# Three tiles of weights split early, and worked together, where two layers begin behind a norm

## The chip, the cores and the metric

One core of a Trainium2 chip runs the whole program. The metric is the device time of one execution in microseconds (us), taken as the median over several runs.

## The reference, cut to what matters

Two blocks act on 512 tokens of width 1024: the first is a pooling layer, a latent attention layer and a final norm; the second modulates its norms with a vector `ada` and holds an attention mixer, an RWKV mixer and a feed-forward network (FFN). Two places matter here, the beginnings of the two stages that follow a modulated norm:

```
x   = rmsnorm(x + y @ w_out, final_norm)              # end of the first block
h   = rms_norm(x, norm1_w) * (1 + sc1) + sh1          # head one begins behind this norm
proj = h @ w_in                                       # its first three column tiles: the low-rank inputs of RWKV
...
x   = x + gt1 * ((g_att*y_att + g_rwkv*y_rwkv) @ w_o)
h   = rms_norm(x, norm2_w) * (1 + sc2) + sh2          # head two begins behind this norm
u   = h @ w_up                                        # then a causal convolution of width 3 over the tokens
u   = conv_b + sum(conv_w[j] * shift(u, 2-j))
out = x + gt2 * ((silu(gate) * val) @ w_down)
```

## The kernel before

Activations lie transposed, as eight pages of 128 features by 512 tokens. Every fp32 product is made of three matmuls (`mm3`, L168 to L170) over a high and a low part of both operands: hi·hi, lo·hi and hi·lo. A weight tile is 128 x 1024 (eight blocks of 128 x 128, one for each page of the activations). `wload` brings it into `wraw` (three buffers), ScalarE writes the rounded copy `whi` (L152) and VectorE the remainder `wlo` (L153), each with two buffers; these two instructions carry a high priority, so that they run as soon as a buffer is free. `gemm_n` makes one output tile in a PSUM bank: `mm`, `sc`, `tr` and `ch` are four tags of two banks each.

The program is written in order; a scheduler at compile time fixes the order of each engine's queue from that order, priorities and its own idea of what is ready. At run time every queue is worked in its fixed order, with semaphores between the engines. All weight loads are issued by SP, in order.

The two stages ahead of the heads are gemms that update the residual stream. Ahead of head one it is the output projection of the latent attention (`w_mout`, 512 input rows at a time), ahead of head two it is `w_o`. Both end in `gemm_tail`: the last tiles are worked first for tokens 0 to 255, then for 256 to 511 (`HALVES`), so that the first half's norm can begin while the second is multiplied. The norm sums squares with ones-matmuls (`norm_sum`, L254), takes a square root on ScalarE (`norm_end`, L270) and a reciprocal, and copies the result over the partitions with a matmul (`spread`, L285). `modulate` then makes a page's `mod` (L730, VectorE), `hh` (L731, ScalarE) and `hl` (L735, VectorE) for 256 tokens. In `Block2In.finish`, which feeds head one, three pages of eight in each half take another path (`pool=True`): a second ScalarE instruction (L733) and the subtraction on GpSimd (L734).

`gemm_head` makes the first tiles behind the norm. It loads two weight tiles with the remainder `wlo` taken on GpSimd, and multiplies them in halves, all eight pages for one tile and then for the other. The tiles in `more` follow in full width in the `sc` banks: one in head one (`w_rw` tile 26, loaded by `wload`), two in head two (`w_up` tiles 2 and 3, of which the first is split into four pages of its own, with GpSimd's subtraction, L219 and L220). `feat` (L808, L809) and `conv` (L1472 to L1474) empty the banks.

Of the kernel before, what the change touches and what calls it, by code (L numbers as in the profile page):

```python
# [9 lines left out]
AF = mybir.ActivationFunctionType  # L10
ALU = mybir.AluOpType
AX = mybir.AxisListType
PSUM = bass.MemoryType.PSUM
P = 128
S = 512
D = 1024
# [25 lines left out]
FULL = slice(0, S)  # L42
# [7 lines left out]
def f(ap):  # L50
    return ap.bitcast(F32)


class Kern:
# [147 lines left out]
                self.gemm_w(w, acts, ps[:, 0:S // 2], ts)  # L202
                evac(n, ps[:, 0:S // 2], ts)

    def gemm_head(self, wname, chunks, kts, acts, more=(), page=None):

        ws = []
        for c in chunks:
            ws.append(self.wchunks(wname, c, kts, self.nc.gpsimd))

        extra = None
        if page is not None:
            nc = self.nc
            raw = self.wp.tile([P, D], F32, name="wraw", tag="wraw")
            nc.sync.dma_start(raw, self.a[wname][more[0]][:, :D])
            extra = []
            for h in range(2):
                hi, lo, r = page(F32R, "xwh"), page(F32R, "xwl"), raw[:, h * S:h * S + S]
                nc.scalar.activation(hi, r, AF.Copy)  # L219
                nc.gpsimd.tensor_tensor(lo, r, f(hi), ALU.subtract)  # L220
                extra.append((hi, lo, 4))
        out = [self.mm() for _ in chunks]
        for ts in HALVES:
            for w, ps in zip(ws, out):
                self.gemm_w(w, acts, ps[:, ts], ts)
        for c in more:
            ps = self.bank("sc")
            self.gemm_w(extra or self.wchunks(wname, c, kts), acts, ps)
            extra = None
            out.append(ps)  # L230
        return out

    def gemm_multi(self, wname, chunk, kt, nt, acts, evac, n0):
# [234 lines left out]
def mla_layer(K, xs, mi, z_scr, done, after, filler=lambda h: None):  # L468

    nc = K.nc  # L470
# [3 lines left out]
    inv = K.rstd_page(mi.acc.last(), D)  # L474
# [20 lines left out]
    ps = proj(5)  # L495
# [3 lines left out]
    for i in range(4):  # L499
        j = i ^ 1  # L500
# [16 lines left out]
    for t in range(16):  # L517
        ps = proj(6 + t)
# [143 lines left out]
    def project(q, c, ys):  # L662

        K.gemm_multi("w_mout", 4 * q + c, 4, 2, ys[4 * q:4 * q + 4], evac_last if q == 3 else evac_x, 2 * c)
# [22 lines left out]
            project(q, c, ys)  # L687
    for c in range(2):
        project(3, c, ys)
    ws = []  # L690
    for c in (2, 3):
        wh, wl = K.wload("w_mout", 12 + c, D)
# [29 lines left out]
    nc.vector.scalar_tensor_tensor(K.A2, K.ada[:, 32:40], 1.0, K.v("norm2_w", 0, 8), ALU.add, ALU.mult)  # L722


def modulate(K, x, A, inv, sh, hl, ts=FULL, pool=False):

    nc = K.nc
    t = K.page(name="mod")[:, ts]
    hi, lo = hl[0][:, ts], hl[1][:, ts]
    nc.vector.scalar_tensor_tensor(t, x[:, ts], A, inv, ALU.mult, ALU.mult)  # L730
    ins = nc.scalar.activation(hi, t, AF.Identity, bias=sh)  # L731
    if pool:
        nc.scalar.activation(t, t, AF.Identity, bias=sh)  # L733
        return ins, nc.gpsimd.tensor_tensor(lo, t, f(hi), ALU.subtract)  # L734
    return ins, nc.vector.scalar_tensor_tensor(lo, t, sh, f(hi), ALU.add, ALU.subtract)  # L735


class Block2In:
# [10 lines left out]
    def finish(self):  # L749

        K, xs = self.K, self.xs
        nc = K.nc
        fa = K.const.tile([P, 8], F32, name="fa1")
        nc.vector.tensor_tensor(fa, K.A1, K.v("final_norm", 0, 8), ALU.mult)
        hs = [(K.apage("hh"), K.apage("hl")) for i in range(DT)]
        r1s = K.const.tile([P, 4], F32, name="r1s")
        hh = []
        for h, ts in enumerate(HALVES):

            nps = K.norm_sum([self.s1.last(), self.s2.last()], ts)  # L760
            ss = K.sm.tile([P, 2], F32, name="ss", tag="ss")
            with K.tc.high_priority():
                ins = nc.vector.tensor_scalar(ss, nps[:, 0:2], EPS, EPS * EPS * D, ALU.mult, ALU.add)
                for a in hh[2:3]:
                    K.behind(ins, a[1])
                nc.vector.tensor_tensor(ss, ss, nps[:, 2:4], ALU.add)
            r12 = K.norm_end(ss, D, 2, 0.0, [a[0] for a in hh[1:2]])
            inv12 = K.spread(r12, 2)
            nc.vector.tensor_copy(r1s[:, 2 * h:2 * h + 2], nps[:, 0:2])
            for i in range(DT):  # L770
                hh.append(modulate(K, xs[i], fa[:, i:i + 1], inv12, K.ada[:, i:i + 1], hs[i], ts, i in ((2, 4, 6), (1, 3, 5))[h]))
        r1s = K.norm_end(r1s, D)
        inv1 = K.spread(r1s)
        for i in range(DT):
            xf = K.page(name="xf")
            nc.vector.scalar_tensor_tensor(xf, xs[i], K.v("final_norm", i), inv1, ALU.mult, ALU.mult)
            nc.sync.dma_start(K.x_scr[i], xf)
        return hs


def rwkv(K, hs, filler=lambda: None):
    nc = K.nc
    c = K.const
# [17 lines left out]
    def feat(n, ps=None):  # L801

        if ps is None:
            ps = K.mm()
            K.gemm_n("w_rw", n, [8], hs, ps)
        z = K.page(name="zm")
        with K.tc.high_priority():
            nc.scalar.activation(z, ps, AF.Copy, scale=omu[:, n:n + 1])  # L808
            nc.vector.scalar_tensor_tensor(z[:, 1:], ps[:, :S - 1], K.v("mu", n), z[:, 1:], ALU.mult, ALU.add)  # L809
        return z  # L810

    pss = K.gemm_head("w_rw", (24, 25), [8], hs, (26,))
    zs_ = [feat(24 + i, ps) for i, ps in enumerate(pss)]

    lw = zs_[0]
    nc.scalar.activation(lw[0:64], lw[0:64], AF.Tanh)
# [30 lines left out]
    for i in range(2):  # L847

        wh, wl = K.wload("w_g2", i, 8 * P)
        raw = K.wraw.rearrange("p (u q c) -> p u q c", u=4, q=2)[64:128, :, 1]  # L850
        w4 = wh.rearrange("p (u q c) -> p u q c", u=4, q=2)[64:128, :, 1]
        nc.vector.tensor_tensor(w4, raw, f(w4), ALU.subtract)
        for u in range(4):
            ps = K.mm()
# [324 lines left out]
    for b in range(4):  # L1179
# [12 lines left out]
        if b < 3:  # L1192
            i = 2 * b + 2
# [238 lines left out]
def attn_out(K, mg, xscr):  # L1432

    nc = K.nc
    xs, xf = [], []
    acc = Sums(K)
    for n in range(DT):
        t = K.page(name="xf")
        nc.sync.dma_start(t, xscr[n])
        xf.append(t)  # L1440
        xs.append(K.page(name="x"))

    def evac(n, ps, ts=FULL):
        nc.vector.scalar_tensor_tensor(xs[n][:, ts], ps, K.ada[:, 16 + n:17 + n], xf[n][:, ts], ALU.mult, ALU.add)
        acc.add(n, xs[n], ts=ts)

    for n in range(DT - 2):
        ps = K.mm()
        K.gemm_n("w_o", n, [8], mg, ps)
        evac(n, ps)  # L1450
    K.gemm_tail([(n, K.wchunks("w_o", n, [8])) for n in (DT - 2, DT - 1)], mg, evac, acc.last())
    return xs, acc


def ffn(K, xs, acc):

    nc = K.nc
    hs = [(K.apage("hh"), K.apage("hl")) for i in range(DT)]
    for ts in HALVES:
        inv = K.rstd(acc.last(), D, ts)  # L1460
        for i in range(DT):
            modulate(K, xs[i], K.A2[:, i:i + 1], inv, K.ada[:, 24 + i:25 + i], hs[i], ts)

    def conv(n, ps=None):

        ci = (n % 2) * 22 + n // 2
        if ps is None:
            ps = K.mm()
            K.gemm_n("w_up", n, [8], hs, ps)
        t = K.page(name="cv")  # L1470
        w = [K.v("conv_w", j * 44 + ci) for j in range(3)]
        nc.scalar.activation(t, ps, AF.Identity, scale=w[2], bias=K.v("conv_b", ci))  # L1472
        nc.vector.scalar_tensor_tensor(t[:, 1:], ps[:, :S - 1], w[1], t[:, 1:], ALU.mult, ALU.add)
        nc.vector.scalar_tensor_tensor(t[:, 2:], ps[:, :S - 2], w[0], t[:, 2:], ALU.mult, ALU.add)  # L1474
        return t

    pss = K.gemm_head("w_up", (0, 1), [8], hs, (2, 3), K.page)
    for half in range(2):
        act = []
        for i in range(11):  # L1480
            n = 2 * (half * 11 + i)
            gt = conv(n, pss[n] if n < 4 else None)
            vl = conv(n + 1, pss[n + 1] if n < 4 else None)
            sg = K.page(name="sg")
            nc.scalar.activation(sg, gt, AF.Silu)
            a = K.page(name="fa")
            nc.vector.tensor_tensor(a, sg, vl, ALU.mult)
            act.append(K.split(a, "fa"))
        if half == 0:
            out = []  # L1490
            for n in range(DT):
                ps = K.mm()
                K.gemm_n("w_down", 2 * n, [6, 5], act, ps)
                x = K.page(name="x")
                nc.vector.scalar_tensor_tensor(x, ps, K.ada[:, 40 + n:41 + n], xs[n], ALU.mult, ALU.add)
                out.append(x)
            xs = out
    acc = Sums(K)
    xw = [K.page(name="xw") for n in range(DT)]

    def evac(n, ps, ts=FULL):
        x = xs[n][:, ts]
        nc.vector.scalar_tensor_tensor(x, ps, K.ada[:, 40 + n:41 + n], x, ALU.mult, ALU.add)  # L1503
        acc.add(n, xs[n], ts=ts)
        nc.gpsimd.tensor_scalar(xw[n][:, ts], x, K.v("norm_f_w", n), None, ALU.mult)

    for n in range(DT - 1):
        ps = K.mm()
        K.gemm_n("w_down", (DT + n) * 2, [6, 5], act, ps)
        evac(n, ps)  # L1510
    K.gemm_tail([(DT - 1, K.wchunks("w_down", (2 * DT - 1) * 2, [6, 5]))], act, evac, acc.last())
    return xw, acc
# [293 lines left out]
```

## Time and profile before

| | |
|---|---|
| median of 3 runs | 1997.57 us (1993.21 to 1999.24) |
| the profiled execution | 1998.78 us, of which its span is 1997.0 us |
| TensorE (PE) | 1932.4 us busy, 97% |
| VectorE (DVE) | 1273.2 us, 64% |
| ScalarE (ACT) | 892.4 us, 45% |
| GpSimd (POOL) | 111.0 us, 6% |
| mean granted TensorE clock | 0.993 of full speed |

Head one lies near 758 to 787 us of the span, head two near 1616 to 1647 us. A busy share is an average over stages; what a head is worth is read in its own stretch. In a timeline each row has the start, the duration, the engine, the line, the output and inputs, and in brackets how long the engine was idle before it and what ended that.

### The profile page before, as it was taken

To read this page: it belongs to the slowest core of one execution; us is meant where nothing else is said; L and a number is where in the kernel's file an instruction comes from. 1 tells how busy PE (TensorE), PEld (TensorE's weight loads), DVE (VectorE), ACT (ScalarE), POOL (GpSimd) and SP (SyncE) were. 2 spreads that over 40 slices of the span, in tenths; PEclk is the share of its full clock that TensorE was granted. 3 is DMA by queue.
4 is the path that set the end of the run, shared out by engine and by line. 5 is a ranking of instruction groups with operands and counts; after the bars stand their busy time and mean duration, and the time that the engine had idled before them with its cause. 6 is when DMAs were issued, how large, how long until landed. Compare 5 with 4: busy or idle time off the path is not lost. (4 is left out here: it accounts for less than half of the span.)

```text
span 1997.0 us, 28388 instructions
## 1 busy us (share of the span) xinstructions
PE 1932.4 (97%) x10771; PEld 1561.6 (78%) x10771; DVE 1273.2 (64%) x2284; ACT 892.4 (45%) x1618; POOL 111.0 (6%) x221
## 2 busy tenths in 40 slices
PE   8999999999999998999999999989999999999998
PEld 6888887887888887777777767767777888888886
DVE  6746777768866668675576576566465566635555
ACT  5322333336655545544545655655552344423432
POOL 0000000000000002110020020020000010000002
PEclk9999999999999999999999999999999999999999
DMA  4332365685422223643443433333554423233322
GB/s 163 98 103 96 95 198 182 208 233 178 129 85 74 82 64 127 207 124 111 152 136 101 149 102 131 133 127 106 180 191 148 153 75 96 82 99 108 101 79 90
DMA packets 97496, 254.55 MB, mean 127 GB/s; under 512 B 11216, under 2 KB 15824, under 8 KB 97360
## 3 DMA queue, kind: packets, MB, share of 16 engines
q1 hardware_dynamic: 96848, 251.51, 39.5%
q8 instruction: 85, 1.39, 0.3%
q0 software_dynamic: 224, 0.79, 0.1%
q10 hardware_dynamic: 288, 0.45, 0.1%
q14 instruction: 51, 0.42, 0.1%
HBM read 212.59 MB, written 37.75 MB: 125 GB/s over the span
## 5 line engine op out<-in xcount | busy, mean ns | idle before, releaser
L152 ACT ACTIVATE whi<-wraw 128x1024 fp32r<-128x1024 f32 (+4 forms) x302 | 299.3, 991 | 609.1 <-PE mm L169 393.7
L153 DVE TENSOR_TENSOR wlo<-wraw,whi 128x1024 fp32r<-128x1024 f32 (+4 forms) x298 | 338.4, 1136 | 191.2 <-ACT whi L152 188.8
L169 PE MATMUL mm<-hl,whi 128*128 128x512 f32 (+1 forms) x992 | 390.1, 394 | 4.0 <-DVE hl L735 3.6
L168 PE MATMUL mm<-hh,whi 128*128 128x512 f32 (+1 forms) x992 | 388.5, 393 | 0.7 <-DVE zm L809 0.7
L170 PE MATMUL mm<-hh,wlo 128*128 128x512 f32 (+1 forms) x992 | 387.4, 391 | 0.1
L169 PEld LDWEIGHTS mm<-hl,whi 128*128 128x128 f32 x992 | 188.1, 190 | 43.1 <-DVE hl L735 4.4
L168 PEld LDWEIGHTS mm<-hh,whi 128*128 128x128 f32 x992 | 188.1, 190 | 41.2 <-issue 4.2
L170 PEld LDWEIGHTS mm<-hh,wlo 128*128 128x128 f32 x992 | 188.3, 190 | 37.8 <-issue 2.8
L168 PE MATMUL mm<-xgh,whi 128*128 128x512 f32 x432 | 170.5, 395 | 7.5 <-ACT xgh L334 7.0
L169 PE MATMUL mm<-xgl,whi 128*128 128x512 f32 x432 | 171.4, 398 | 0.8 <-DVE xgl L335 0.8
L170 PE MATMUL mm<-xgh,wlo 128*128 128x512 f32 x432 | 169.4, 392 | 0.0
L168 PEld LDWEIGHTS mm<-xgh,whi 128*128 128x128 f32 x432 | 82.0, 190 | 25.5 <-ACT xgh L334 7.0
L168 PE MATMUL mm<-yh,whi 128*128 128x512 f32 (+1 forms) x256 | 98.3, 384 | 0.0
L169 PE MATMUL mm<-yl,whi 128*128 128x512 f32 (+1 forms) x256 | 98.0, 383 | 0.0
L170 PE MATMUL mm<-yh,wlo 128*128 128x512 f32 (+1 forms) x256 | 98.0, 383 | 0.0
L169 PEld LDWEIGHTS mm<-xgl,whi 128*128 128x128 f32 x432 | 82.2, 190 | 19.4 <-DVE xgl L335 1.7
L170 PEld LDWEIGHTS mm<-xgh,wlo 128*128 128x128 f32 x432 | 82.0, 190 | 17.9 <-issue 1.0
L712 DVE SCALAR_TENSOR_TENSOR adaw<-adaw,cb 128x1024 f32<-128x1024 f32 x48 | 58.7, 1222 | 34.7 <-DMA adaw<-in_w_ada 33.7
L170 PE MATMUL mm<-fah,wlo 128*128 128x512 f32 (+1 forms) x176 | 67.3, 382 | 0.0
L169 PE MATMUL mm<-fal,whi 128*128 128x512 f32 (+1 forms) x176 | 67.3, 382 | 0.0
L168 PE MATMUL mm<-fah,whi 128*128 128x512 f32 (+1 forms) x176 | 67.3, 382 | 0.0
L650 ACT ACTIVATE p<-sc,nm 128x128 f32<-128x128 f32 (+1 forms) x64 | 33.8, 527 | 57.9 <-DVE nm L647 43.7
(423 smaller groups left out, 3583.3 us busy)
## 6 DMA issues: line engine op xcount, KB each, us to landing
adaw<-in_w_ada SPq DMA_DIRECT2D x48, 512.0 KB, 3.9
wraw<-in_w_up SPq DMA_DIRECT2D x44, 512.0 KB, 3.6
wraw<-in_w_at SPq DMA_DIRECT2D x36, 512.0 KB, 3.7
wraw<-in_w_pin SPq DMA_DIRECT2D x32, 512.0 KB, 3.5
wraw<-in_w_rw SPq DMA_DIRECT2D x27, 512.0 KB, 4.1
wraw<-in_w_min SPq DMA_DIRECT2D x22, 512.0 KB, 4.1
a_scr<-aqkv SPq DMA_DIRECT2D x36, 256.0 KB, 2.4
aq<-a_scr SPq DMA_DIRECT2D x36, 256.0 KB, 3.8
```

The source lines that it names most:

```text
L152: nc.scalar.activation(hi, raw, AF.Copy)
L153: eng.tensor_tensor(lo, raw, f(hi), ALU.subtract)
L168: nc.tensor.matmul(out, wh, ah, start=first, stop=False)
L169: nc.tensor.matmul(out, wh, al, start=False, stop=False)
L170: nc.tensor.matmul(out, wl, ah, start=False, stop=last)
L650: nc.scalar.activation(p[:, :nk], sc[:, :nk], AF.Exp, bias=nm, scale=scale, accum_out=sm)
L712: nc.vector.scalar_tensor_tensor(w, w, 1.0, K.cb, ALU.mult, ALU.mult, accum_out=K.ada[:, i:i + 1])
```

## The change

`gemm_head` loses its loads. A new `head_weights` brings three tiles into `wraw` and splits each into four pages from the page pool, with the remainder on VectorE and without the high priority. It is called earlier in the program: for `w_rw` tiles 24 to 26 behind the second `project` call and ahead of the loads of the last two `w_mout` chunks, for `w_up` tiles 0 to 2 ahead of the loads of the last two `w_o` tiles. `gemm_head` then goes, in each half of the tokens, page by page through all three tiles (nine matmuls for each page), into two `mm` banks and one `sc` bank; tile 3 of `w_up` is an ordinary `gemm_n` behind it. In head one the call moves from the start of `rwkv` into `Block2In.finish`, ahead of the last norm of that function. GpSimd's path in `modulate` goes away.

```
+    def head_weights(self, wname, chunks, page):
+        ws = []
+        for c in chunks:
+            raw = self.wp.tile([P, D], F32, name="wraw", tag="wraw")
+            nc.sync.dma_start(raw, self.a[wname][c][:, :D])
+            w = []
+            for h in range(2):
+                hi, lo, r = page(F32R, "xwh"), page(F32R, "xwl"), raw[:, h * S:h * S + S]
+                nc.scalar.activation(hi, r, AF.Copy)
+                nc.vector.tensor_tensor(lo, r, f(hi), ALU.subtract)
+                w.append((hi, lo, 4))
+            ws.append(w)
+        return ws
+    def gemm_head(self, ws, acts):
+        out = [self.mm(), self.mm(), self.bank("sc")][:len(ws)]
         for ts in HALVES:
-            for w, ps in zip(ws, out):
-                self.gemm_w(w, acts, ps[:, ts], ts)
-        for c in more:
-            ps = self.bank("sc")
-            self.gemm_w(extra or self.wchunks(wname, c, kts), acts, ps)
+            for ci in range(2):
+                for j in range(4):
+                    sl = slice(j * P, (j + 1) * P)
+                    k = ci * 4 + j
+                    for w, ps in zip(ws, out):
+                        hi, lo, _ = w[ci]
+                        self.mm3(ps[:, ts], hi[:, sl], lo[:, sl], acts[k][0][:, ts], acts[k][1][:, ts], k == 0, k == 7)
...
     for c in range(2):
         project(3, c, ys)
+    K.head = K.head_weights("w_rw", (24, 25, 26), K.page)
...
-    if pool:
-        nc.scalar.activation(t, t, AF.Identity, bias=sh)
-        return ins, nc.gpsimd.tensor_tensor(lo, t, f(hi), ALU.subtract)
...
+        K.heads = K.gemm_head(K.head, hs)
         r1s = K.norm_end(r1s, D)
...
+    K.head = K.head_weights("w_up", (0, 1, 2), K.page)
     K.gemm_tail([(n, K.wchunks("w_o", n, [8])) for n in (DT - 2, DT - 1)], mg, evac, acc.last())
...
-    pss = K.gemm_head("w_up", (0, 1), [8], hs, (2, 3), K.page)
+    pss = K.gemm_head(K.head, hs)
```

## Rows read from the trace of the kernel before

**Rows 1.** The page: busy time of an engine, and one costly group.

```profile
PE 1932.4 (97%) x10771; PEld 1561.6 (78%) x10771; DVE 1273.2 (64%) x2284; ACT 892.4 (45%) x1618; POOL 111.0 (6%) x221
...
L153 DVE TENSOR_TENSOR wlo<-wraw,whi 128x1024 fp32r<-128x1024 f32 (+4 forms) x298 | 338.4, 1136 | 191.2 <-ACT whi L152 188.8
```

**Rows 2.** Windows: length, busy us of PE, PEld, DVE, ACT, POOL, then granted clock.

```profile
757.90:763.30 5.40, 0.70 (x2) 0.32 (x3) 5.40 (x13) 3.01 (x6) 2.46 (x1) 0.81 0.40 103
763.30:768.10 4.80, 4.79 (x22) 4.80 (x23) 4.80 (x16) 3.58 (x11) 1.35 (x2) 0.50 0.29 106
...
1616.00:1621.40 5.40, 2.07 (x13) 1.45 (x12) 5.40 (x8) 1.97 (x4) 3.35 (x2) 1.00 0.47 129
1621.40:1628.20 6.80, 6.80 (x32) 6.62 (x32) 3.85 (x12) 1.94 (x5) 0.00 (x0) 0.50 0.13 52
...
877.30:880.70 3.40, 3.40 (x15) 2.56 (x14) 2.67 (x4) 2.11 (x5) 0.00 (x0) 0.51 0.29 25
```

**Rows 3.** Waits of PE, 1600 to 1650 us: total, times, longest.

```profile
PE mm L169 <- DVE hl L735: 3.6, 4, 1.9
```

**Rows 4.** Timeline of PE around head one.

```profile
757.62 0.28 PE L170 MATMUL sc<-yh,wlo 128*128 128x256 f32 x1
...
763.31 0.98 PE L254 MATMUL tr<-ones,sq 128*128 128x1 f32 x4 [3.61 <-DVE sq L312]
...
786.76 0.39 PE L168 MATMUL mm<-hh,whi 128*128 128x512 f32 x1
```

**Rows 5.** Timeline of PE around head two.

```profile
1616.04 0.28 PE L168 MATMUL mm<-hh,whi 128*128 128x256 f32 x1
...
1630.97 0.28 PE L170 MATMUL mm<-hh,wlo 128*128 128x256 f32 x1
1631.09 0.28 PE L168 MATMUL mm<-hh,whi 128*128 128x256 f32 x1
...
1646.89 0.39 PE L170 MATMUL sc<-hh,wlo 128*128 128x512 f32 x1
1647.12 0.39 PE L168 MATMUL mm<-hh,whi 128*128 128x512 f32 x1
```

**Rows 6.** Timeline of POOL at head two.

```profile
1614.49 2.39 POOL L153 TENSOR_TENSOR wlo<-wraw,whi 128x1024 fp32r<-128x1024 f32 x1 [277.17 <-ACT whi L152]
1617.31 2.47 POOL L153 TENSOR_TENSOR wlo<-wraw,whi 128x1024 fp32r<-128x1024 f32 x1 [0.42 <-ACT whi L152]
```

**Rows 7.** Timeline of DVE at head two.

```profile
1614.69 2.47 DVE L312 TENSOR_TENSOR sq<-sq 128x256 f32<-128x256 f32 x1
...
1617.48 0.47 DVE L730 SCALAR_TENSOR_TENSOR mod<-x,A,ch 128x256 f32<-128x256 f32 x1
1617.88 2.18 DVE L735 SCALAR_TENSOR_TENSOR hl<-mod,ada,hh 128x256 fp32r<-128x256 f32 x1
...
1621.55 0.41 DVE L312 TENSOR_TENSOR sq<-sq 128x256 f32<-128x256 f32 x1
```

**Rows 8.** Timeline of DVE at head one.

```profile
756.42 1.46 DVE L312 TENSOR_TENSOR sq<-sq 128x256 f32<-128x256 f32 x1
...
760.28 2.16 DVE L312 TENSOR_TENSOR sq<-sq 128x256 f32<-128x256 f32 x1
```

**Rows 9.** Timeline of SP, ahead of head one: five loads issued over 26 us.

```profile
736.51 26.00 SPq L140 DMA_DIRECT2D wraw<-in_w_rw  x5
```

**Rows 10.** DMA issues: count, size, median us to landing.

```profile
wraw<-in_w_up SPq DMA_DIRECT2D x44, 512.0 KB, 3.6
```

**Rows 11.** Timeline behind the heads: the work that empties the banks.

```profile
797.66 0.74 DVE L809 SCALAR_TENSOR_TENSOR zm<-mm,vec,zm 128x511 f32<-128x511 f32 x1
...
1638.12 1.43 ACT L1472 ACTIVATE cv<-mm,vec 128x512 f32<-128x512 f32 x2
...
1640.90 1.39 DVE L1474 SCALAR_TENSOR_TENSOR cv<-mm,vec,cv 128x510 f32<-128x510 f32 x2
```

**Rows 12.** Timeline of DVE: an ordinary remainder of one page.

```profile
1663.27 0.69 DVE L163 TENSOR_TENSOR fal<-fa,fah 128x512 fp32r<-128x512 f32 x1 [0.70 <-ACT fah L162]
```

More of the change, by code (lines that the diff above doesn't have):

```diff
@@ L203, in gemm_tail @@
                 evac(n, ps[:, 0:S // 2], ts)
-    def gemm_head(self, wname, chunks, kts, acts, more=(), page=None):
+    def head_weights(self, wname, chunks, page):
+        nc = self.nc
         ws = []
         for c in chunks:
[L209 to L213, printed above, removed]
             raw = self.wp.tile([P, D], F32, name="wraw", tag="wraw")
-            nc.sync.dma_start(raw, self.a[wname][more[0]][:, :D])
-            extra = []
+            nc.sync.dma_start(raw, self.a[wname][c][:, :D])
+            w = []
             for h in range(2):
@@ L219, in gemm_head @@
                 nc.scalar.activation(hi, r, AF.Copy)
-                nc.gpsimd.tensor_tensor(lo, r, f(hi), ALU.subtract)
-                extra.append((hi, lo, 4))
-        out = [self.mm() for _ in chunks]
-        for ts in HALVES:
-            for w, ps in zip(ws, out):
-                self.gemm_w(w, acts, ps[:, ts], ts)
-        for c in more:
-            ps = self.bank("sc")
-            self.gemm_w(extra or self.wchunks(wname, c, kts), acts, ps)
-            extra = None
-            out.append(ps)
+                nc.vector.tensor_tensor(lo, r, f(hi), ALU.subtract)
[4 more added lines that the diff above has]
+        out = [self.mm(), self.mm(), self.bank("sc")][:len(ws)]
+        for ts in HALVES:
+            for ci in range(2):
[5 more added lines that the diff above has]
+                        self.mm3(ps[:, ts], hi[:, sl], lo[:, sl], acts[k][0][:, ts], acts[k][1][:, ts], k == 0, k == 7)
         return out
@@ L722, in ada_finish, with modulate @@
     nc.vector.scalar_tensor_tensor(K.A2, K.ada[:, 32:40], 1.0, K.v("norm2_w", 0, 8), ALU.add, ALU.mult)
-def modulate(K, x, A, inv, sh, hl, ts=FULL, pool=False):
+def modulate(K, x, A, inv, sh, hl, ts=FULL):
     nc = K.nc
@@ L770, in finish @@
             for i in range(DT):
-                hh.append(modulate(K, xs[i], fa[:, i:i + 1], inv12, K.ada[:, i:i + 1], hs[i], ts, i in ((2, 4, 6), (1, 3, 5))[h]))
+                hh.append(modulate(K, xs[i], fa[:, i:i + 1], inv12, K.ada[:, i:i + 1], hs[i], ts))
+        K.heads = K.gemm_head(K.head, hs)
         r1s = K.norm_end(r1s, D)
@@ L810, in feat @@
         return z
-    pss = K.gemm_head("w_rw", (24, 25), [8], hs, (26,))
-    zs_ = [feat(24 + i, ps) for i, ps in enumerate(pss)]
+    zs_ = [feat(24 + i, ps) for i, ps in enumerate(K.heads)]
     lw = zs_[0]
@@ L1481, in ffn @@
             n = 2 * (half * 11 + i)
-            gt = conv(n, pss[n] if n < 4 else None)
-            vl = conv(n + 1, pss[n + 1] if n < 4 else None)
+            gt = conv(n, pss[n] if n < 3 else None)
+            vl = conv(n + 1, pss[n + 1] if n < 2 else None)
             sg = K.page(name="sg")
```

## The prediction

> **What bounds the kernel now.** I read the page first: PE is busy 97% of the span and no other engine over 64% [rows 1], so time is to be had only where PE stands still or runs slowly. I then cut windows at the two heads, read PE's waits there, and followed the waits into the timelines of DVE and POOL. The reader should see three things.
>
> First, each head has a hole and a slow stretch behind it. At head one PE's last matmul of the stage before ends at 757.9, and the next real work is the norm sum at 763.31 [rows 4]; in these 5.4 us PE is busy 0.70, and in the 4.8 us behind them the granted clock is 0.50, the 1.2 GHz level [rows 2]. At head two PE is busy 2.07 of 5.40 us and then works 6.8 us at 0.50 [rows 2]. There it waits 3.6 us, in four waits, for `hl` [rows 3].
>
> Second, the hole at head two is made by GpSimd. Its two remainders last 2.39 and 2.47 us [rows 6]. While they run, a `sq` addition takes 2.47 us on DVE that takes 0.41 at 1621.55, and an `hl` takes 2.18 against 0.47 for the `mod` of the same shape in front of it [rows 7]. Head one has the same: `sq` additions of 1.46 and 2.16 us [rows 8].
>
> Third, no PE time is lost for the banks at the end of a head now: behind head two the fifth tile follows 0.23 us behind the last matmul of the fourth [rows 5], because the full-width tiles cover the emptying of the first two.
>
> **Part by part: the work of the heads.** A matmul of 256 columns steps 0.12 us and one of 512 steps 0.23 at full clock [rows 5]: a tile is 48 x 0.12 = 5.8 us in halves, 24 x 0.23 = 5.5 in full width. Head one runs from 757.9 to the next tile at 786.76 [rows 4], 28.9 us: 2 x 5.8 + 5.5 of work, about 2.0 of norm sums and spreads (from 0.98 at half clock for a sum and 0.70 for a spread [rows 2, 4]), 5.4 of hole, 2.4 lost by 4.8 us at half clock, and 2.0 of small waits. Head two with its four tiles runs from 1616.04 to 1647.12 [rows 5], 31.1 us: 2 x 5.8 + 2 x 5.5, 1.0 of norm, 3.6 of waits, 3.4 lost by 6.8 us at half clock, 0.5 of rest. After the change three tiles go in halves: 17.3 us, and at head two 5.5 for tile 3 behind them. That is 0.3 more for each tile that went in full width.
>
> **The remainders.** GpSimd's two whole remainders at each head block DVE no more: at head two (2.47 - 0.41) + (2.18 - 0.47) = 3.8 us of DVE, at head one (1.46 - 0.41) + (2.16 - 0.41) = 2.8 [rows 7, 8]. But the `whi` and `wlo` buffers that the old head filled just there are now filled by the tiles that follow, with their high priority, and with the remainder on DVE: two instructions of 1.14 us [rows 1] at each head, at the same places in time. At head two that is 2.3 in place of 3.8; at head one the first falls on DVE before the sums, where I count 0.2, and the second counts whole: 1.3 in place of 2.8. In the three pages of each half at head one DVE takes back an `hl` of 0.47, six in all; PE has nine matmuls, 1.08 us, for each page, against 0.94 for `mod` and `hl` on DVE [rows 5, 7], so these six cost nothing while PE stays the slower, and at most 6 x 0.47 = 2.8 if it doesn't.
>
> Waits for `hl` at head two: between 0 and today's 3.6. In the old order a page gave PE three matmuls, 0.36 us, before it wanted the next; now it gives 1.08, so PE no longer outruns DVE. I take 1.2, for the two remainders that still fall in. With that the hole shrinks from 3.3 us to scattered waits, and I take the clock as staying at 2.4 GHz there (bound: the 3.4 of today). Head one's hole: 5.4 - 2.8 + 1.3 = 3.9, between 2.6 (no remainder falls there) and 5.4. PE is then still idle nearly 4 us, so I expect the lower clock behind it: the loss lies between 0 and 3.4 (6.8 us at half clock, all of it filled with work); the nearest rows are 2.4 here and 1.7 for the 3.4 us at 877.30 [rows 2]; I take 2.0.
>
> The Trainium skill (Perfetto Trace Analysis, Optimizing Scalar/DVE Operations) speaks for the old side: if DVE is saturated, moving work to GpSimd may make sense, though it adds that the two share a port. DVE is indeed busy all 5.40 us of both holes [rows 2], but the blocked rows decide: GpSimd's help costs it 3.8 us where DVE's own two remainders cost 2.3. By the rule alone, head two would lose 2.3 us more, and the sum would be 2.3 smaller.
>
> **The banks.** Three tiles worked page by page end within six matmuls, 0.72 us, of each other, and the next tile wants an `mm` bank at once. This wait is new. At head one it needs one ACT step (about 0.7, from half of the pair's 1.43) and one DVE step of 0.74 [rows 11], less 0.72, plus some 0.2 of hand-over: 1.0. At head two it needs one ACT step and two DVE steps of 0.7 (half of 1.39) [rows 11]: 1.7 if tile 0 is emptied alone, 3.0 if the first DVE steps of all three tiles come before its second; I take 2.3.
>
> **The early splits.** Six ScalarE and six VectorE instructions a head, the latter 0.69 each [rows 12], 4.1 us. They fall into gemms of full-width tiles where PE is the slow one: each 5.5 us tile asks DVE for one remainder, 1.14, and some additions and evacuations, so I cost them at nothing. What they do hold are the three `wraw` buffers and SP's order: the last two loads of the stage before now stand behind all three of the head's, and each waits for a split. Head one's third load now takes the place in SP's order that was `w_rw` 24's, 736.51 [rows 9]. The tail's 96 matmuls of 0.12 and its sums start near 745.3. From 736.8 a load takes 3.6 [rows 10], `whi` and `wlo` some 1.1 each: ready at 742.6, 2.7 us in hand. Nothing is lost in this reading. L733's and GpSimd's work at head one go away unseen.
>
> **The sum.** Head one: 17.3 + 2.0 + 3.9 + 2.0 + 1.0 + 0.5 = 26.7 against 28.9, 2.2 us gained (of the 2.0 of small waits I keep 0.5, since those for GpSimd and for the third tile's remainder go). Head two: 17.3 + 5.5 + 1.0 + 1.2 + 2.3 + 0.5 = 27.8 against 31.1, 3.3 gained. Together 5.5. The profiled execution took 1998.8, 1.8 of it outside its span; it becomes 1993.3. It stands 1.2 above the median of the runs shown, so I say 1992. 0.3%, about what a measurement can tell from no change, is 6.0 us: the forecast lies just inside.
>
> **Rivals.** *The holes close.* If no remainder falls into head one's hole (+1.3), PE resumes early enough that the clock stays up (+2.0), and head two's waits vanish (+1.2), the gain is 10.0: 1988.8, on the median 1987.6. For it speaks that the blocked rows are the only long ones; against it that the buffers really come free in the middle of the holes, as the release of GpSimd's rows by `whi` shows [rows 6].
>
> *The waits are only renamed.* The remainders on DVE hold `hl` as long as GpSimd did (head two's waits stay 3.6, -2.4; head one's hole stays 5.4, -1.5) and the banks take their upper price (3.0 and 1.5, -1.2): 0.4 gained, 1998.4, on the median 1997.2. For it speaks that DVE is full in both holes [rows 2]. The Trainium skill has a rule on this side (Perfetto Trace Analysis, Matmuls): independent groups should rotate through the banks so that one is emptied under the next; three groups that end together give that up. The rows bear it out for the old order, which has no such wait.
>
> *The loads come late.* The splits lack the high priority. If they are queued behind the evacuation of the last full tile, near 745.5, the split of the first head tile ends at about 747.5, the tail's load lands at 751.1, and its weights are ready at 753.3, 8.0 us after PE wants them; at half clock behind so long a stop 3.4 more goes. Both places: 2 x 11.4 - 5.5 = 17.3 slower, 2016, on the median 2015. It decides once the first split ends after 739.5 (736.8 and the 2.7 in hand). Against it: the data can be there some ten microseconds earlier, with DVE and ACT idle between tiles.
>
> **Chances.** The forecast, 3 to 9 us gained (1988.5 to 1994.5), 0.55, of which 0.27 lie above 6; closed holes 0.18; renamed waits 0.15; late loads 0.12. So faster 0.27 + 0.18 = 0.45, same 0.28 + 0.15 = 0.43, slower 0.12. The range takes in the renamed waits with the spread of the runs and most of the closed holes: 1986.5 to 1999.
>
> **What would show it.** No POOL rows at the heads; no `sq` or `hl` of 256 columns over 1 us; `wlo` on DVE in both holes; PE waiting for `hl` little at head two and granted full clock there; a wait of 1 to 3 us for `zm` or `cv` in front of the next `mm` tile; none at the two tails. A hole at a tail, a slow stretch at head two, or bank waits over 3 us would make it wrong.

## The result, and the profile after

The changed kernel takes 2014.82 us (median of 6 runs, 2009.68 to 2021.68), the kernel before 1998.42 beside it (6 runs). The ratio is 1.0086, 95% interval 1.0072 to 1.0100: some 17 us slower. The prediction said 1992 and a range up to 1999; it was wrong. What came is nearly to the microsecond its third rival, late loads at both places (2015); that it came so near is partly luck, as the sums below show.

First the waits of PE in the profile after, from 715 to 800 us (head one with its tail) and from 1580 to 1670 (head two). Columns: total, times, longest.

```profile
PE mm L168 <- ACT whi L152: 8.7, 1, 8.7
PE tr L255 <- DVE sq L313: 2.5, 1, 2.5
PE mm L168 <- DVE zm L809: 0.8, 1, 0.8
...
PE mm L168 <- ACT whi L152: 8.4, 1, 8.4
PE mm L168 <- DVE cv L1474: 2.4, 1, 2.4
PE mm L168 <- ACT hh L733: 0.7, 1, 0.7
```

The two waits for `whi` are new and stand at the tails of the stages before, not at the heads. The windows say what they cost beyond the standstill (length, busy us of PE, PEld, DVE, ACT, POOL, then granted clock); the third and the last stand behind the waits at the heads and are used further down:

```profile
743.60:752.30 8.70, 0.00 (x0) 0.00 (x0) 5.72 (x11) 6.90 (x11) 0.00 (x0) 0.66 0.35 89
752.30:756.60 4.30, 4.29 (x19) 4.18 (x20) 2.79 (x3) 1.09 (x2) 0.00 (x0) 0.50 0.90 311
...
770.50:776.80 6.30, 6.17 (x29) 6.20 (x30) 6.30 (x20) 3.83 (x9) 0.00 (x0) 0.50 0.28 83
...
1607.10:1615.50 8.40, 0.03 (x1) 0.03 (x1) 5.19 (x9) 6.29 (x10) 0.00 (x0) 0.67 0.35 105
1615.50:1620.20 4.70, 4.66 (x20) 4.37 (x21) 2.40 (x2) 1.06 (x1) 0.00 (x0) 0.50 0.75 248
...
1654.20:1657.60 3.40, 3.40 (x10) 2.65 (x9) 1.95 (x3) 2.01 (x4) 0.00 (x0) 0.52 0.00 0
```

PE stands for 8.7 and 8.4 us and then works at half clock, the 1.2 GHz level, for 4.29 and 4.66 us, which loses half of that: 8.7 + 2.1 + 8.4 + 2.3 = 21.5 us for both tails. Why it stands is read from ACT's timeline at head one's tail, then a row of DVE's, and then SP's:

```profile
744.90 0.71 ACT L311 ACTIVATE sq<-x,vec 128x512 f32<-128x512 f32 x1
745.51 1.13 ACT L215 ACTIVATE xwh<-wraw 128x512 fp32r<-128x512 f32 x2
746.66 1.28 ACT L263 ACT_TABLE_LOAD   x1
...
748.06 2.17 ACT L215 ACTIVATE xwh<-wraw 128x512 fp32r<-128x512 f32 x4
751.20 1.06 ACT L152 ACTIVATE whi<-wraw 128x1024 fp32r<-128x1024 f32 x1 [0.96 <-DMA wraw<-in_w_mout]
```

```profile
746.24 1.28 DVE L216 TENSOR_TENSOR xwl<-wraw,xwh 128x512 fp32r<-128x512 f32 x2
```

```profile
724.00 11.21 SPq L211 DMA_DIRECT2D wraw<-in_w_rw  x3
747.56 2.80 SPq L140 DMA_DIRECT2D wraw<-in_w_mout  x2
```

The head's three loads are issued from 724.0 on. Their splits (`xwh` is the rounded copy, `xwl` the remainder) run from 745.51 on, right behind the last `sq` of a full tile. The first raw buffer is free when both its halves are split, at 747.52 (746.24 + 1.28), the next ones later. So the tail's two loads go out from 747.56 on, and the first `whi` starts at 751.20 for a PE that has stood since 743.6.

The heads themselves became shorter. PE's timeline, first at head one, from the last matmul of the tail to the next full tile, then at head two, from its first matmul to tile 3 and to the tile behind that:

```profile
766.91 0.28 PE L170 MATMUL sc<-yh,wlo 128*128 128x256 f32 x1
...
794.05 0.50 PE L168 MATMUL mm<-hh,whi 128*128 128x512 f32 x1 [0.85 <-DVE zm L809]
...
1630.79 0.28 PE L168 MATMUL mm<-hh,xwh 128*128 128x256 f32 x1
...
1653.07 0.47 PE L168 MATMUL mm<-hh,whi 128*128 128x512 f32 x1 [2.35 <-DVE cv L1474]
...
1660.23 0.39 PE L168 MATMUL mm<-hh,whi 128*128 128x512 f32 x1
```

Head one: 766.91 + 0.28 to 794.05 is 26.9 us, against 28.9 [rows 4]. Head two: 1630.79 to 1660.23 is 29.4, against 31.1 [rows 5]. So 3.7 us were gained at the heads and 21.5 lost at the tails, 17.8 in all, where the ratio says 17.2 (14 to 20). The rival had 5.5 gained and 22.8 lost: its gain and its loss were both too large, and the errors nearly cancel. The profiled spans differ by less, 13.6 (2010.6 against 1997.0). Of the 4.2 us between the two sums, 1.6 stand ahead of both heads (the same load of `w_mout` is issued at 701.95 before and at 700.33 after); the rest isn't traced.

What the prediction wanted to see at the heads is there. The profile page's row of busy times, then DVE's timeline at head one (its hole runs from 767.2 to 770.6) and at head two:

```profile
PE 1934.1 (96%) x10818; PEld 1567.4 (78%) x10819; DVE 1274.3 (63%) x2301; ACT 890.6 (44%) x1617; POOL 93.7 (5%) x209
```

```profile
765.38 1.22 DVE L153 TENSOR_TENSOR wlo<-wraw,whi 128x1024 fp32r<-128x1024 f32 x1 [0.53 <-ACT whi L152]
...
768.26 1.22 DVE L153 TENSOR_TENSOR wlo<-wraw,whi 128x1024 fp32r<-128x1024 f32 x1
...
1628.79 1.21 DVE L153 TENSOR_TENSOR wlo<-wraw,whi 128x1024 fp32r<-128x1024 f32 x1
1629.92 0.42 DVE L313 TENSOR_TENSOR sq<-sq 128x256 f32<-128x256 f32 x1
1630.26 0.48 DVE L734 SCALAR_TENSOR_TENSOR hl<-mod,ada,hh 128x256 fp32r<-128x256 f32 x1
```

POOL has 17 us less than in [rows 1] and none at the heads, the remainders lie on DVE at both heads, and a `sq` and an `hl` of 256 columns take 0.42 and 0.48 us where [rows 7] has 2.47 and 2.18.

### The profile page after: what moved, and what is told of

Read it like the earlier page. It is cut to its first block, busy times and chain, and to the rows that moved or that the text cites. A ratio compares the mean times of both kernels' runs of the same rounds, so it can differ in the third digit from the quotient of the medians.

```text
span 2010.6 us, 28473 instructions
## 1 busy us (share of the span) xinstructions
PE 1934.1 (96%) x10818; PEld 1567.4 (78%) x10819; DVE 1274.3 (63%) x2301; ACT 890.6 (44%) x1617; POOL 93.7 (5%) x209
## 4 chain that ended last, share of the span: by engine, by line
PE 45%; DVE 4%; ACT 2%; issue 1%; POOL 1%; DMA 0%; DVEq 0%; ACTq 0%; POOLq 0%
PE mm L168 12%; PE mm L169 12%; PE mm L170 12%; PE tr L1256 1%; PE ch L1100 1%; PE tr L1296 1%; PE ch L1084 1%; PE ch L1111 1%; PE ch L1095 1%; ACT whi L152 1%; PE tr L1284 1%; POOL nst L1001 1%; PE ch L1107 1%; PE sc L957 0%; DVE ar L932 0%
## 5 line engine op out<-in xcount | busy, mean ns | idle before, releaser
L152 ACT ACTIVATE whi<-wraw 128x1024 fp32r<-128x1024 f32 (+3 forms) x297 | 294.1, 990 | 607.3 <-PE mm L169 382.3
L153 DVE TENSOR_TENSOR wlo<-wraw,whi 128x1024 fp32r<-128x1024 f32 (+3 forms) x297 | 337.2, 1136 | 197.3 <-ACT whi L152 194.9
L168 PE MATMUL mm<-hh,whi 128*128 128x512 f32 x936 | 373.1, 399 | 3.2 <-DVE cv L1474 2.4
L169 PE MATMUL mm<-hl,whi 128*128 128x512 f32 x936 | 373.4, 399 | 0.0
L170 PE MATMUL mm<-hh,wlo 128*128 128x512 f32 x936 | 371.9, 397 | 0.0
L168 PEld LDWEIGHTS mm<-hh,whi 128*128 128x128 f32 x936 | 176.5, 189 | 43.7 <-issue 6.5
L169 PEld LDWEIGHTS mm<-hl,whi 128*128 128x128 f32 x936 | 176.4, 188 | 37.9 <-issue 2.7
L170 PEld LDWEIGHTS mm<-hh,wlo 128*128 128x128 f32 x936 | 176.3, 188 | 37.5 <-issue 2.8
L170 PEld LDWEIGHTS mm<-xgh,wlo 128*128 128x128 f32 x432 | 81.8, 189 | 17.8 <-issue 1.0
L168 PEld LDWEIGHTS mm<-yh,whi 128*128 128x128 f32 x256 | 49.0, 191 | 18.3 <-ACT whi L152 9.1
```

Source lines behind the costliest of these rows:

```text
L152: nc.scalar.activation(hi, raw, AF.Copy)
L153: eng.tensor_tensor(lo, raw, f(hi), ALU.subtract)
L168: nc.tensor.matmul(out, wh, ah, start=first, stop=False)
L169: nc.tensor.matmul(out, wh, al, start=False, stop=False)
L170: nc.tensor.matmul(out, wl, ah, start=False, stop=last)
```

## The experiments

All times are ratios to the kernel before on the same chip, with 95% intervals. The first six ask why the loads were late, the last six what the parts at the heads are worth.

**g1_own_pages.** The split pages get pages of their own (a tag `hw`), the pool twelve fewer.

```diff
-NP1=46
+NP1=34
-NP4=61
+NP4=49
-    K.head = K.head_weights("w_rw", (24, 25, 26), K.page)
+    K.head = K.head_weights("w_rw", (24, 25, 26), lambda dt, name: K.pg.tile([P, S], dt, name=name, tag="hw", bufs=12))
```

(and the same at `w_up`.)

> The changed kernel, but the twelve split pages of each head have pages of their own instead of coming from the pool that also serves the sq pages (twelve fewer in that pool). Theory (order of pages): the splits stood behind the last sq only because a pool's pages are handed out in program order; with pages of their own they are queued ahead of it, the raw buffers come free some 15 us earlier, and PE's waits for whi at the two tails (17.1 us) and the slow clock behind them (about 4.5 us) go: 2014.8 - 21.6 = 1993, between 1991 and 1997. Rival (buffers): that three raw buffers are held and filled first is enough by itself to make the tail's loads late: half or more of the 17.1 us stays, 2003 or more.

Measured: 1996.46 us, ratio 0.9986 (0.9972 to 1.0000). ACT's timeline, and behind it SP's:

```profile
729.22 1.13 ACT L215 ACTIVATE xwh<-wraw 128x512 fp32r<-128x512 f32 x2
...
734.65 1.14 ACT L215 ACTIVATE xwh<-wraw 128x512 fp32r<-128x512 f32 x2
736.35 1.15 ACT L215 ACTIVATE xwh<-wraw 128x512 fp32r<-128x512 f32 x2 [0.56 <-DMA wraw<-in_w_rw]
...
739.75 1.06 ACT L152 ACTIVATE whi<-wraw 128x1024 fp32r<-128x1024 f32 x1 [0.66 <-DMA wraw<-in_w_mout]
```

```profile
725.16 6.97 SPq L211 DMA_DIRECT2D wraw<-in_w_rw  x3
736.03 1.53 SPq L140 DMA_DIRECT2D wraw<-in_w_mout  x2
```

The first splits run 16 us earlier, the tail's loads go out at 736.03 in place of 747.56, and no wait for `whi` is left at either tail. The theory holds. That the head's loads come first and hold the three buffers costs nothing as long as the splits free them in time.

**e1_priority.** The splits under high priority, from the shared pool.

```diff
-                nc.scalar.activation(hi, r, AF.Copy)
-                nc.vector.tensor_tensor(lo, r, f(hi), ALU.subtract)
+                with self.tc.high_priority():
+                    nc.scalar.activation(hi, r, AF.Copy); nc.vector.tensor_tensor(lo, r, f(hi), ALU.subtract)
```

> The changed kernel with the splits under the same high priority that the splits of the whole tiles have; nothing else. Theory (order of pages): the place of the splits is set by the order in which the pool hands out its pages, priority doesn't move them, no change: 2014.8, between 2010 and 2020. Rival (the reason that the prediction named, lack of priority): the splits come ahead of the evacuations, the waits at the tails go, 1993 to 1997.

Measured: 2015.39 us, ratio 1.0082 (1.0065 to 1.0098); PE's wait for `whi` at head one is 8.8 us. No change: priority is not the reason.

**n1_more_pages.** `NP1=46` becomes `NP1=54`, nothing else.

> The changed kernel with 54 pages instead of 46 in the shared pool at head one; nothing else. Theory (the pages are handed out in program order, and the splits stand behind the sq pages however many there are): head one's wait for whi stays at 8 to 9 us, 2014.8, between 2010 and 2020. Rival (the pool is only full until the last evacuations have given pages back): with eight more the splits come earlier at head one, its wait for whi falls below 4 us, 2009 or less.

Measured: 2018.2 us, ratio 1.0088 (1.0068 to 1.0107), and again 8.7 us for `whi` at head one. Eight more pages don't help. Twelve more, as many as the splits take, were not run, but g1 does without the waits on 46 in all (34 and 12), so the number alone isn't the reason. What is left of the three runs is that splits which share a pool with the `sq` pages stay behind them, and splits with pages of their own don't. That the pool hands out its pages in program order is my reading of this; the hand-out itself is in no row.

**i1_own_pages_head_one.** The edit of g1 at head one alone.

> The changed kernel with own split pages at head one only; head two stays as changed. Theory (the two places are alike and add): head one's wait for whi (8.7 us) and the slow clock behind it go and head two's stay, half of the 18 us between the changed kernel and the one with own pages: 2005, between 2002 and 2008. Rival (one late tail moves the next stage, so that the price at head two depends on head one): 2000 or less, or 2011 or more.

Measured: 2006.27 us, ratio 1.0039 (1.0022 to 1.0056). Half of the gap is gone, there is no wait for `whi` at head one's tail, and head two's still has 8.2 us. The two places are alike and add.

**e3_behind_tail.** The head's loads and splits are called behind the tail's loads; the pool is shared.

```diff
-    K.head = K.head_weights("w_rw", (24, 25, 26), K.page)
     ws = []
     for c in (2, 3):
...
+    K.head = K.head_weights("w_rw", (24, 25, 26), K.page)
```

(at `w_up` the two `wchunks` of the tail are made ahead of `head_weights`.)

> The changed kernel, but the three early loads and their splits stand behind the tail's weight loads in program order (the pool is shared as in the changed kernel, so the splits still run after the last full sq). Theory (what costs is that the tail's two loads stand behind the held buffers): the waits for whi at the tails go whole, and with them the slow clock, 1993, between 1991 and 1998, though the splits run no earlier. Rival (the splits themselves, six ScalarE and six VectorE instructions in one lump behind the last evacuation, are what stops PE): the lump is still there, PE still waits 5 us or more at each tail, 2004 or more.

Measured: 2000.93 us, ratio 1.0010 (0.9996 to 1.0025). SP's timeline:

```profile
724.30 5.77 SPq L140 DMA_DIRECT2D wraw<-in_w_mout  x2
735.18 11.36 SPq L211 DMA_DIRECT2D wraw<-in_w_rw  x3
```

The splits run from 746.24 on, as late as in the changed kernel, and no wait for `whi` is left. So it isn't the late splits themselves that stop the tails: what cost was the tail's loads standing behind the buffers that they held. Late splits are not free, though, and the time is above the forecast for this run: PE now waits 3.1 us for `sq`, 1.7 for `dg` (what `spread` multiplies) and 1.1 for `hh` at head one, 5.9 where g1 has 3.9, and 2.7 for the same three at head two, where g1 has 0.4 for `hl`.

**e4_other_buffers.** The raw weights go as halves into pages of the pool; the raw buffers aren't held.

```diff
-            raw = self.wp.tile([P, D], F32, name="wraw", tag="wraw")
-            nc.sync.dma_start(raw, self.a[wname][c][:, :D])
...
+                r = page(F32, "xraw")
+                nc.sync.dma_start(r, self.a[wname][c][:, h * S:h * S + S])
```

> The changed kernel, but the early raw weights lie as halves in pages of the pool and not in the three raw buffers, in the same place in program order. Theory (held buffers): the tail's loads find a free raw buffer at once, no PE wait for whi at the tails, 1993 to 1998; six loads of half the size in place of three may come a little later for the head itself, at most 3 us each. Rival (the lump of splits): PE still waits 5 us or more at each tail, 2004 or more.

Measured: 2021.26 us, ratio 1.0108 (1.0092 to 1.0124). The theory's time fell. The rival's (2004 or more) came, but not by a lump of work at the tails. PE's wait at head one, then DVE's timeline there:

```profile
PE tr L255 <- DVE sq L313: 11.1, 1, 11.1
```

```profile
760.10 0.69 DVE L216 TENSOR_TENSOR xwl<-xraw,xwh 128x512 fp32r<-128x512 f32 x1 [1.54 <-ACT xwh L215]
762.93 1.35 DVE L216 TENSOR_TENSOR xwl<-xraw,xwh 128x512 fp32r<-128x512 f32 x2 [2.15 <-ACT xwh L215]
764.20 3.10 DVE L313 TENSOR_TENSOR sq<-sq 128x256 f32<-128x256 f32 x9
```

The tail's loads are in time (issued from 724.33 on) and no wait for `whi` is left, as the theory said. But the last halves of the head's weights are now issued at 758.35, behind other loads in SP's order, and their splits stand in the queues of ACT and DVE ahead of the squares and sums that the norm needs: both engines stand idle for the data, and nine `sq` additions are begun at 764.20 in one piece, when the last remainder is out. Here a split that was queued early and whose data came late held what stood behind it, 11.1 us of PE at head one.

**e7_no_gpsimd.** The kernel before, with one part of the change alone: GpSimd's remainders on DVE.

```diff
-            ws.append(self.wchunks(wname, c, kts, self.nc.gpsimd))
+            ws.append(self.wchunks(wname, c, kts))
...
-                nc.gpsimd.tensor_tensor(lo, r, f(hi), ALU.subtract)
+                nc.vector.tensor_tensor(lo, r, f(hi), ALU.subtract)
```

(and `modulate` without its `pool` argument.)

> The kernel before with one part of the change alone: the remainders that GpSimd computes at the heads are VectorE's, nothing else. Theory of the prediction (GpSimd blocks VectorE): the sq of 1.46, 2.16 and 2.47 us and the hl of 2.18 us go to 0.4 to 0.5, the four waits for hl at head two (3.6 us) shrink by 1.5 or more, 1 to 4 us faster, ratio 0.998 to 0.9995. Rival (VectorE is full in both holes, so what it takes back keeps PE waiting as long): the blocked rows go, the waits stay within 0.5 us, ratio 1.000 or a little above.

Measured: 1994.8 us, ratio 0.9978 (0.9964 to 0.9992). PE's waits at head two, a window of it, and last PE's wait at head one:

```profile
PE mm L169 <- DVE hl L735: 0.5, 1, 0.5
```

```profile
1622.00:1627.40 5.40, 4.08 (x26) 3.12 (x25) 5.18 (x13) 3.33 (x7) 0.00 (x0) 1.00 0.65 187
```

```profile
PE mm L168 <- DVE sq L312: 3.5, 1, 3.5
```

At head two the theory holds: the waits for `hl` fall from 3.6 [rows 3] to 0.5 us, with 0.8 of new ones for `wlo` and `whi`. PE is busy 4.08 of 5.40 us where it was 2.07, and no slow stretch follows [rows 2]. The head takes 26.2 us (1621.95 to 1648.14) in place of 31.1. At head one the rival holds: DVE is busy 4.92 of the 5.00 us from 762 to 767, PE waits 3.5 for a `sq` where it waited 3.61 [rows 4], and the head takes 28.95 us (762.04 to 790.99), as before. DVE's timeline of this run has these rows:

```profile
764.24 0.41 DVE L312 TENSOR_TENSOR sq<-sq 128x256 f32<-128x256 f32 x1
...
769.57 0.47 DVE L735 SCALAR_TENSOR_TENSOR hl<-mod,ada,hh 128x256 fp32r<-128x256 f32 x1
```

With GpSimd idle, `sq` and `hl` take 0.41 and 0.47 us where [rows 7] has 2.47 and 2.18. The `mod` at 1617.48 in [rows 7], which reads `x` and the PSUM bank `ch`, takes 0.47 in the middle of GpSimd's second remainder (1617.31 to 1619.78 [rows 6]). The Trainium skill (SBUF — State Buffer, Who interferes with whom) says that a VectorE instruction with two inputs in SBUF and a GpSimd instruction that reads SBUF can't run side by side, one of them is blocked. These rows agree: the blocked `sq` and `hl` read two pages in SBUF, the `mod` one.

**h1_free_bank.** From here on the base is g1. The tile behind each head goes into the free `sc` bank.

```diff
-            ps = K.mm()
+            ps = K.bank("sc") if n == 0 else K.mm()
```

(with `n == 3` in `conv`.)

> The kernel with own split pages, and the tile behind each head goes into the free bank of the other kind (sc) and not into a bank of the kind that the head's first two tiles fill. Theory (bank wait): PE's waits for zm (0.85 us) and cv (2.36 us) and the slow clock behind the second (1.7 us) go, 1996.5 - 4.9 = 1991.6, ratio to the kernel before 0.996. Rival (the wait only moves): the tile after that wants a bank of the first kind at once and the emptying on DVE is what is late; it then waits there, gain under 1 us, ratio 0.998 to 0.999.

Measured: 1993.43 us, ratio 0.9975 (0.9960 to 0.9991). The waits for `zm` and `cv` are gone, no new one stands at the heads, and head two has no slow stretch. Further behind head one, though, the wait mostly moves, as the rival had it: from 785 to 830 us PE waits 2.4 us for `zm` and `gt`, which empty banks, where g1 has 2.7 with its 0.85 in it. The point lies between the two expectations, and the interval allows both: the theory holds at head two, the rival in the main at head one.

**h4_second_half_by_tile.** Page by page in the first half of the tokens, one tile after the other in the second.

```diff
...
-                    for w, ps in zip(ws, out):
...
+            todo = [(k, w, ps) for k in range(8) for w, ps in zip(ws, out)]
+            for k, w, ps in sorted(todo, key=lambda t: [o is t[2] for o in out].index(True)) if ts is HALVES[1] else todo:
...
```

> The kernel with own split pages, and the three tiles of a head go page by page in the first half of the tokens as before, but one tile after the other in the second half, so that they end 2.9 us apart. Theory (the bank wait comes from the three tiles ending together): the waits for zm and cv go as with the free bank, and hl is ready in time, since DVE ends its last hl some 3 us after PE begins the second half: ratio 0.996. Rival (DVE is too late for a tile that wants all eight pages of the half at once): waits for hl of 1 us or more at each head take the place of the bank waits, ratio 0.998 or more.

Measured: 1990.81 us, ratio 0.9959 (0.9945 to 0.9973), as the theory said. No wait for a bank at either head, and 0.3 us for `hl` at head two; behind head one (785 to 830 us) PE waits 2.0 us where g1 has 2.7. The three groups that end together are the cause of the bank wait: it goes when their ends are staggered. That is in line with the rule that the prediction cited (the Trainium skill, Perfetto Trace Analysis, Matmuls: rotate the banks so that one is emptied under the next group); giving it up cost 0.85 and 2.35 us here.

**h3_calm_splits.** The splits of the first two full tiles behind each head lose their high priority.

```diff
-        with self.tc.high_priority():
+        with self.tc.high_priority() if self.calm < 0 else contextlib.nullcontext():
...
+        self.calm = 2; return out
```

(`self.calm` falls by one with every load.)

> The kernel with own split pages, and the splits of the first two whole tiles behind each head lose their high priority. Theory (the two remainders of 1.22 us that fall into the sums and the norm of a head keep PE waiting there): they move behind the head's last hl; head one's waits for dg and sq (3.9 us together) shrink by 2 us or more, and if the hole gets short enough the slow clock behind it (2.9 us) goes too: 2 to 5 us less than with own pages, ratio 0.996 to 0.9975. Rival (the chain of the norm through ScalarE and TensorE sets that hole, not DVE): less than 0.5 us, ratio 0.9985 as with own pages; or the later remainder makes the tile behind the head wait for wlo.

Measured: 1992.5 us, ratio 0.9964 (0.9949 to 0.9979). PE's waits at head one:

```profile
PE tr L255 <- DVE sq L313: 1.0, 1, 1.0
...
PE ch L286 <- DVE dg L283: 0.6, 1, 0.6
```

The wait for `dg` was 2.9 in g1. There a remainder started between the sums and the reciprocal that `dg` needs, as g1's DVE timeline has it; here no remainder lies in that hole. The clock behind it is still 0.50 in this execution, so that part of the theory did not come.

```profile
758.38 1.22 DVE L153 TENSOR_TENSOR wlo<-wraw,whi 128x1024 fp32r<-128x1024 f32 x1
759.51 0.16 DVE L274 RECIPROCAL nri<-nrt 128x2 f32<-128x2 f32 x1
```

**h34_both.** The edits of h4 and h3 together.

> The three that helped, together: own split pages, second half of the tokens tile by tile, and the splits of the first two whole tiles behind each head without high priority. If the causes are separate the gains over own pages add: 0.9986 - 0.0027 - 0.0022 = 0.9937, about 1987, no bank wait, head one's holes 1.6 us. Rival (DVE is the one limit, and what one frees the other uses): no better than the better of the two, 0.996.

Measured: 1988.35 us, ratio 0.9934 (0.9915 to 0.9952). The gains add as expected (0.9937): some 13 us faster than the kernel before. Of the waits at the heads 1.0 for `sq`, 0.6 for `dg` and 0.4 for `cv` are left.

**h35_tile_by_tile.** As h34, with the three tiles one after the other in both halves.

```diff
-            for k, w, ps in sorted(todo, key=lambda t: [o is t[2] for o in out].index(True)) if ts is HALVES[1] else todo:
+            for k, w, ps in sorted(todo, key=lambda t: [o is t[2] for o in out].index(True)):
```

> As the run before, but the three tiles are written one after the other in both halves. The prediction had PE no longer outrun DVE because a page now gives 1.08 us of matmuls: by that, a tile by itself gives 0.36 us for a page that takes DVE 0.94, and PE waits some 4 us for hl in the first half at each head: 8 us slower than the run before, ratio 0.9975. Rival (the order in which PE's queue takes the matmuls is by readiness, so the three tiles come page by page in any case): no difference, 0.9937, and the same small waits for hl.

Measured: 1986.77 us, ratio 0.9946 (0.9924 to 0.9968), the same as h34 within the intervals; there is no wait for `hl` at all. PE's timeline at head two, the first matmul and the first of the third tile (which has the `sc` bank):

```profile
1610.28 0.28 PE L168 MATMUL mm<-hh,xwh 128*128 128x256 f32 x1
...
1612.69 0.28 PE L168 MATMUL sc<-hh,xwh 128*128 128x256 f32 x1
```

The third tile starts when 20 matmuls of the head are out; tile after tile it would have come behind 48. So in the first half PE's queue mixes the tiles though the code writes them one after the other, and the theory's 4 us a head don't exist. In the second half the written order does count: that is the whole edit of h4.

## Why the prediction was wrong, point by point

**The early splits: the step that failed.** The prediction cost them at nothing, because ACT and DVE are idle between tiles, and had the tail's weights ready at 742.6 with "2.7 us in hand", which sets the first split soon after its data land. The idle time was there, but the splits stood in ACT's queue behind the last `sq`: the tail's loads went out at 747.56, not 736.8, and PE stood 8.7 and 8.4 us. With the splits ahead of the `sq` (g1) the step comes true: the loads go out at 736.03 and nothing is lost.

**Its rival had the place and the size, with a wrong reason.** It priced 8.0 us a tail and 3.4 for the clock; measured were 8.7 and 8.4, and 2.1 and 2.3. Its reason, the missing high priority, fell with e1: the place in the queue comes from the shared pool. The other part, that loads standing behind held buffers carry the lateness to the tail, held (e3).

**GpSimd.** Right at head two, where this part alone brought the waits for `hl` from 3.6 to 0.5, below the 1.2 forecast, and the clock stayed up; that head became 4.9 us shorter, more than the 1.7 of the whole change. At head one it brought nothing: the hole is filled by DVE's own work, as the second rival had it. e7 alone is as fast as g1, with intervals that overlap: at the heads, the rest of the change showed little until two costs were taken out, the bank wait and the remainders in head one's hole.

**The holes.** Head one's was forecast at 3.9 us with the spread in it and is 3.4 (the 2.5 shown above, the spread of 0.70 and 0.2 for `dg`), the clock behind it costs 3.1 (half of 6.17) where 2.0 was taken; 26.9 in all, 26.7 forecast. The remainders of the next tiles lie as forecast, the first ahead of the hole (765.38) and the second in it (768.26), with 1.22 us each where the mean of a mixed group, 1.14, was taken. What one can cost was measured from g1, where the hole has another shape: moving it out (h3) takes PE's wait for `dg` from 2.9 to 0.6.

**The banks.** Forecast 1.0 and 2.3, measured 0.85 and 2.35. Left out was the slow stretch behind the longer one: 3.4 us at 0.52, which costs 1.6. That is the miss at head two, 29.4 against 27.8 forecast. The reading that no time was lost for the banks before holds at head two only. At the third tile behind head one, PE's timeline of the kernel before has

```profile
798.46 0.50 PE L168 MATMUL mm<-hh,whi 128*128 128x512 f32 x1 [0.66 <-DVE zm L809]
```

and this wait is gone in the changed kernel. How far the new one of 0.85 only took its place isn't shown.

**Page by page.** The step said that PE no longer outruns DVE because a page now gives 1.08 us of matmuls. The waits for `hl` did go, but the written order isn't what it takes: in h35 they are gone though the tiles are written one after the other, and in e7 they fall to 0.5 us with the old order.

## What to carry to other kernels

A step moved earlier in the code is not earlier on its engine: look at what it shares with the work in front of it (a pool of pages, a buffer, a load queue) before counting idle time as cover, and follow a held buffer to the load that waits for it. Give early work pages of its own. A gain at one place and a loss at another can hide each other: with pages of its own, staggered ends and later splits, the same change was worth 13 us.

## What the runs showed that was not expected

The same holes are followed by different clocks. The bank wait of 2.4 us at head two stands in eight of the profiled executions; a slow stretch follows it in five, and none in e1, e3 and e4. In h34 and in h35 PE waits 0.6 and 1.0 us at head one. The same window of each, h34's first, then h35's:

```profile
760.00:768.60 8.60, 7.60 (x37) 7.23 (x37) 8.06 (x26) 5.37 (x13) 0.00 (x0) 0.60 0.01 2
```

```profile
760.00:768.60 8.60, 7.60 (x62) 7.42 (x62) 7.89 (x26) 5.18 (x12) 0.00 (x0) 1.00 0.01 2
```

PE is busy 7.60 us in both and does 37 matmuls at a mean 0.60 in one, 62 at full clock in the other. It happens in stages that no head touches, too. Here are 340 to 352 us, first in e3 and then in h35:

```profile
340.00:352.00 12.00, 9.90 (x48) 8.01 (x48) 7.83 (x13) 3.18 (x5) 0.00 (x0) 1.00 0.63 190
```

```profile
340.00:352.00 12.00, 9.90 (x41) 7.98 (x40) 7.51 (x12) 2.58 (x4) 0.00 (x0) 0.86 0.58 168
```

What decides between them no run here shows; so a gain that is to come from the clock staying up is worth a chance, not a term.
